# Emitting the S5 table pieces over three projections instead of in one go after the first

## The chip, the core and the metric

One core of a Trainium2 chip runs the whole program. The metric is device time in microseconds (us) of one execution, as the median of several runs; less is better. The engines that matter are TensorE (PE: matmuls, and beside it PEld, its weight loads), VectorE (DVE), ScalarE (ACT), GpSimd (POOL) and SyncE (SP, which issues the weight transfers). Each works through its own list of instructions in order and waits for the others through semaphores.

## The reference, cut to what matters

The program is one layer of a decoder for 256 tokens with 2048 features: a token mixer, cross-attention into a memory, and a gated MLP. Only the mixer's beginning is touched here. It projects the input with one matrix and splits the columns into an S5 state-space group, stick-breaking attention heads, and the heads of a third kind of attention (NSA).

```python
proj = h @ w_in
(u5, sq, sk, sv, nq, kc, vc, ksl, vsl, ksw, vsw, g) = jnp.split(proj, offsets, axis=-1)
y_s5 = s5_mixer(u5, lam_re, lam_im, log_dt, b_re, b_im, c_re, c_im, d, w_glu, b_glu)
y_sb = stick_breaking(heads(sq, SB_HEADS), heads(sk, SB_HEADS), heads(sv, SB_HEADS))
...
# s5_mixer: a complex diagonal recurrence over time, then a gated unit
_, _, sr, si = lax.associative_scan(_complex_affine, (a_r, a_i, xr_in, xi_in), axis=1)
y = einsum(sr, c_re) - einsum(si, c_im) + d * uf
z = jax.nn.gelu(y)
out = z * jax.nn.sigmoid(z @ w_glu + b_glu)
# stick_breaking, per head
w = jnp.where(mask, jnp.exp(jax.nn.log_sigmoid(z) + later), 0.0)
```

The kernel turns the complex recurrence into a real one: it rotates the inputs by a table of cosines and sines over time, runs two real scans with the decay's magnitude, and rotates back. These cosine and sine tables (128 states by 16 groups by 256 steps each) are the "S5 tables".

## The kernel before, in words

Every projection streams its weights from memory in chunks of 512 KB (128 partitions by 1024 numbers; the gates' ones are smaller). `weights` (L272 on) issues the load of a chunk, and `split_chunk` splits it: ScalarE casts a high part (`hi`, L304), VectorE subtracts to get the low part (`lo`, L305). There are four buffers for raw chunks and three each for `hi` and `lo`. Each weight tile then takes three matmuls on TensorE (`mm3`, L319 to L321, with 256 columns, output by features; `mm3x`, L327 to L329, output by tokens): `hi` times the high input, `hi` times the low input, `lo` times the high input. Results lie in three PSUM buffers named `pj`.

The order of the projections: S5's input (`load_x`, 8 chunk pairs); the stick-breaking values (8 chunks, by tokens); queries and keys of the stick-breaking heads (16 chunks: for each of four head pairs t two of queries, two of keys); four column groups for compressed keys and values (8 chunks, `nsa_compress`); NSA values and gates (4 chunks and 8 smaller ones, `nsa_values`); NSA keys (4 + 4 chunks, `nsa_keys`); then the gated unit of S5 (`s5_out`, two chunks of `w_glu`, 48 matmuls from the tiles `s5zs`); then the NSA queries (16 chunks).

Beside them runs a background: the generator `s5_work`, which `step` advances by one piece. `weights` adds `self.pace` to a credit for each chunk and emits a piece for each whole credit. The pieces in order: 4 that build the input matrices (`s5_inputs`: `s5t`, `s5lb`, transposes into `mx`), 32 of the tables (four quarters of 8 pieces: ScalarE fills `Es` and `Ec` with phases, VectorE reduces them in two pieces, ScalarE takes an absolute value and two sines), then 66 of the recurrence. When the first of these last is emitted, the pace becomes 2.8. A state of the recurrence (16 in all) is four pieces: TensorE gives the input product `pb`, VectorE multiplies (`s5m`), adds (`s5z`), scans twice (also into `s5z`), multiplies again and writes `Ec` and `Es`; after every fourth state TensorE forms the output `pa` and VectorE adds it to `s5u`. All have line L191, a helper that issues the engine call and places it behind the latest weight split (VectorE, ScalarE) or a recent projection matmul (TensorE).

The pace is set to 0.8 in `load_x` when its fourth chunk is loaded. After the values, `stick_breaking` has a loop, `while len(self.sins) < 4: self.step()`, that emits all table pieces that are left: 9 of 36 are out by then and 27 follow at once. Then comes the load of ScalarE's table for exponential and logarithm, which has to stand behind the last sine, and the queries and keys. The attention of each head pair t follows (scores in `mx`, `sbe` on ScalarE, `sbs` on VectorE, sums by TensorE into the same `mx`, the weighted values in `op`). `s5_out` emits what is left of the background before it starts on the gelu.

The program names priorities by lane, and a scheduler sets the final order on each engine from these priorities and the dependencies; so a change of where a piece is emitted can move many instructions.

Of the kernel before, what the change touches and what calls it, by code (L numbers as in the profile page):

```python
# [36 lines left out]
SKEW = 16  # L37
MOVING_AT = {512: 48, 256: 32}
NORM0, NORM1, HOLD = 3, (2,), 2
TABLE_PACE, SCAN_PACE = 0.8, 2.8  # L40
BUCKET_FROM = [16, 21, 27, 35, 46, 59, 77, 99, 128, 166, 216]


# [122 lines left out]
class Parts:  # L166
# [9 lines left out]
    def range(self, k, n):  # L176
        if k == 0 and self.first is not None:
            assert n == 1
            return self.first
        return self.tiles[k // self.n][:, k % self.n:k % self.n + n]  # L180
# [18 lines left out]
class Program:  # L199
# [263 lines left out]
    def load_x(self):  # L463

        nc, a, S = self.nc, self.a, self.nc.scalar
        raw = self.slabp.tile([128, KD, 256], F32, name="xraw", tag="Es")
        self.s5u = u = self.s5p.tile([128, 4, 256], F32, name="s5u")
        ps = [self.pj.tile([128, 512], F32, name="pj") for _ in range(3)]
        ps.append(self.op.tile([128, 512], F32, name="op"))
        for c in range(8):  # L470
            s = slice(2 * c, 2 * c + 2)
            with self.lane("split"):
                nc.sync.dma_start(raw[:, s, :], a["xT"][:, s, :])
                self.split_to(self.Xt[:, s, 0, :], self.Xt[:, s, 1, :], raw[:, s, :])
            n = 1 if c == 0 else 2
            for j in range(0, 2, n):
                hi, lo = self.weights(a["win_u"][0, c, :, 512 * j:512 * (j + n)], 512 * n)
                for i in range(n):
                    k = 2 * c + j + i
                    for t in range(4):  # L480
                        w = slice(512 * i + 128 * t, 512 * i + 128 * t + 128)
                        self.mm3(ps[t][:, :256], hi[:, w], lo[:, w], self.X(k, 0), self.X(k, 1),
                                 k == 0, k == KD - 1)
            with self.lane("split"):
                if c == CST_AT:
                    nc.sync.dma_start(self.cst, a["cst"])
                    nc.sync.dma_start(self.bmat, a["s5b"])
                    self.pace = TABLE_PACE
                if c == 7:
                    nc.sync.dma_start(self.cmat, a["s5c"])  # L490

        self.s5us = self.s5p.tile([96, 16, 256], F32R, name="s5us")
        parts = self.Ec[:, 8:16, :].bitcast(F32R).rearrange("p (i t) c -> p i t c", i=2)
        for t in range(4):
            S.copy(u[:, t, :], ps[t][:, :256])
            self.split_to(parts[:, 0, t, :], parts[:, 1, t, :], ps[t][:, :256])
        for j, i in enumerate((0, 1, 0)):
            self.stack(nc.gpsimd, self.s5us[32 * j:32 * j + 32], parts[:, i])

        self.ident16, self.smask16 = (  # L500
            self.s5p.tile([128, 128], mybir.dt.bfloat16, name=f"m16{i}") for i in range(2))
        S.copy(self.ident16, self.ident)
        S.copy(self.smask16, self.smask)
        S.activation(self.nident, self.ident, ACTF.Copy, scale=-1.0)
# [299 lines left out]
    def stick_breaking(self):  # L804
        nc, a, V, S = self.nc, self.a, self.nc.vector, self.nc.scalar
        q = self.sbp.tile([128, 4, 256], F32, name="sbq")
        k = self.sbp.tile([128, 4, 256], F32, name="sbk")
        v = self.sbp.tile([128, 2, 512], F32, name="sbv")
        for i, ps in enumerate(self.to_cols(a["win_sv"][0], self.X, 512, 2, 0, KD)):
            S.copy(v[:, i, :], ps)  # L810
        while len(self.sins) < 4:
            self.step()
        table = self.exp_ln_table(self.sins)
        for t in range(4):
            ps = self.to_rows(a["win_c"], t, self.X)
            S.activation(q[:, t, :], ps, ACTF.Copy, scale=HD ** -0.5)
            ps = self.to_rows(a["win_c"], 4 + t, self.X)
            V.tensor_copy(k[:, t, :], ps)
        self.nsa_bias()
        mm, values = nc.tensor.matmul, []  # L820
        for t in range(4):
            ops = self.op.tile([128, 512], F32, name="op")

            halves = [slice(64 * hh, 64 * hh + 64) for hh in range(2)]
            zs = [self.mx.tile([128, 512], F32, name="mx") for _ in halves]
            row = []
            for c in range(2):
                for z, rows in zip(zs, halves):
                    row.append(mm(z[:, 256 * c:384 if c else 256],
                                  k[rows, t, 128 * c:128 * c + 128], q[rows, t, 128 * c:256],  # L830
                                  start=c == 0, stop=False))
            for z in zs:
                row.append(mm(z[:, 0:128], self.ident16, self.smask16, start=False, stop=False))
                row.append(mm(z[:, 256:384], self.ident16, self.smask16, start=False, stop=True))
            self.in_row(values[-1:] + row)
            ws, exps = [], []
            for z in zs:
                e = self.sbw.tile([128, 384], F32, name="sbe")
                sp = self.sbw.tile([128, 384], F32, name="sbs")
                S.activation(e, z[:, :384], ACTF.Abs)  # L840
                self.after(S.activation(e, e, ACTF.Exp, scale=-1.0), table)
                S.activation(e, e, ACTF.Ln, bias=1.0)
                V.scalar_tensor_tensor(sp, z[:, :384], 0.0, e, ALU.max, ALU.add)
                mm(z[:, 0:384], self.ntri, sp, start=False, stop=False, skip_group_check=True)
                mm(z[:, 128:256], self.nones, sp[:, 256:384], start=False, stop=True,
                   skip_group_check=True)
                w = self.sbw.tile([128, 384], F32, name="sbe")
                exps.append(S.activation(w, z[:, :384], ACTF.Exp))
                self.sb_exp = exps[-1]
                ws.append(w)  # L850
            row = values = []
            for c, (k0, k1) in enumerate(((0, 256), (256, 384))):
                for hh, (w, rows) in enumerate(zip(ws, halves)):
                    h = 2 * t + hh
                    row.append(mm(ops[rows, 128 * c:256], v[:, c, 64 * h:64 * h + 64], w[:, k0:k1],
                                  start=c == 0, stop=c == 1))
            self.tc.add_manual_dep(row[0].ins, exps[1].ins.name, mybir.DependencyInfo(
                mybir.DependencyClass.Sync, mybir.DependencyReason.DATA), reason="side by side")
            self.in_row(row)
            S.copy(self.mix[1][:, t, 0, :], ops[:, :256])  # L860
            V.tensor_sub(self.mix[1][:, t, 1, :], ops[:, :256],
                         self.mix[1][:, t, 0, :].bitcast(F32))
# [507 lines left out]
```

## Time and profile before

| What | us |
|---|---|
| Median of 3 runs | 1277.29 (1276.85 to 1277.38) |
| The profiled execution's own time | 1276.8 |
| Its span in the profile | 1274.6 |
| TensorE busy | 1242.8 |
| TensorE's weight loads busy | 1151.6 |
| VectorE busy | 878.8 |
| ScalarE busy | 660.5 |

The times of the profile are from the start of its span. A busy time counts the union of an engine's instructions; successive instructions overlap by a little, so a row of equal ones is better read from start to start. A group's line names the source line, the engine, the operation, and output and input by the program's names.

### The profile page before, as it was taken

Reading aid. Unit: us, or ns where it says so; the run is one execution under the profiler, and the core shown is the slowest. Engines: PE = TensorE matmul, PEld = TensorE weight load, DVE = VectorE, ACT = ScalarE, POOL = GpSimd, SP = SyncE. Lnnn points to the kernel's source line nnn. Section 1 sums busy time; section 2 is a strip of 40 time slices with the busy share of each in tenths; the row PEclk is TensorE's granted clock in tenths of the full one; section 3 lists DMA queues with packets and bytes.
Section 4 is the critical chain, followed back from the end, with each engine's and each line's share of the span. In section 5 each row is a group of like instructions: output and inputs, shape, how many; then the busy total and the mean of one; then the engine's idle time right before and its main releaser. Section 6 shows DMA issues by size and latency. Waiting matters only on the chain.

```text
span 1274.6 us, 23037 instructions
## 1 busy us (share of the span) xinstructions
PE 1242.8 (98%) x9222; PEld 1151.6 (90%) x9222; DVE 878.8 (69%) x1507; ACT 660.5 (52%) x1032; POOL 19.0 (1%) x34
## 2 busy tenths in 40 slices
PE   7999999999999999899999999999999999999996
PEld 7788889997788999799999999999999988888896
DVE  7799997876765766866666666666666654444557
ACT  6884446565663366365555555555555543334342
POOL 0200000100000000000000000000000000000000
PEclk9999999999999999999999999999999999999998
DMA  8654247664454655355666666666566766656573
GB/s 307 196 167 150 84 130 239 213 197 141 133 204 160 193 196 169 113 164 191 196 192 192 196 193 191 196 194 190 196 192 192 262 192 190 196 188 199 187 237 132
DMA packets 67350, 237.37 MB, mean 186 GB/s; under 512 B 7787, under 2 KB 8604, under 8 KB 66476
## 3 DMA queue, kind: packets, MB, share of 16 engines
q1 hardware_dynamic: 64720, 230.21, 55.9%
q0 software_dynamic: 1424, 4.33, 1.5%
q8 instruction: 72, 1.18, 0.4%
q10 hardware_dynamic: 1100, 1.38, 0.3%
q14 instruction: 34, 0.28, 0.1%
HBM read 231.82 MB, written 2.49 MB: 184 GB/s over the span
## 4 chain that ended last, share of the span: by engine, by line
PE 86%; DVE 6%; DMA 3%; ACT 3%; issue 2%; POOL 0%; DVEq 0%; ACTq 0%; POOLq 0%
PE pj L321 16%; PE pj L319 16%; PE pj L320 16%; PE pj L328 10%; PE pj L327 10%; PE pj L329 10%; PE pa L1081 2%; DVE s5m L191 1%; DVE lo L305 1%; DMA s5us<-Ec 1%; DVE s5z L191 1%; DMA raw<-in_win_u 1%; ACT hi L304 1%; PE mx L1044 1%; PE mx L1045 1%
## 5 line engine op out<-in xcount | busy, mean ns | idle before, releaser
L305 DVE TENSOR_TENSOR lo<-raw,hi 128x1024 fp32r<-128x1024 f32 (+2 forms) x403 | 488.1, 1211 | 330.4 <-ACT hi L304 329.2
L304 ACT CAST hi<-raw 128x1024 fp32r<-128x1024 f32 (+2 forms) x403 | 419.6, 1041 | 500.2 <-PE pj L320 268.1
L320 PE MATMUL pj<-mix,hi 128*128 128x256 f32 x1380 | 382.4, 277 | 0.0
L319 PE MATMUL pj<-mix,hi 128*128 128x256 f32 x1380 | 381.9, 277 | 0.0
L321 PE MATMUL pj<-mix,lo 128*128 128x256 f32 x1380 | 381.3, 277 | 0.0
L319 PEld LDWEIGHTS pj<-mix,hi 128*128 128x128 f32 x1380 | 259.5, 188 | 0.2
L320 PEld LDWEIGHTS pj<-mix,hi 128*128 128x128 f32 x1380 | 259.4, 188 | 0.1
L321 PEld LDWEIGHTS pj<-mix,lo 128*128 128x128 f32 x1380 | 259.4, 188 | 0.0
L319 PE MATMUL pj<-A,hi 128*128 128x256 f32 x496 | 139.6, 284 | 6.7 <-ACT hi L304 6.1
L321 PE MATMUL pj<-A,lo 128*128 128x256 f32 x496 | 137.6, 284 | 3.7 <-DVE lo L305 3.7
L320 PE MATMUL pj<-A,hi 128*128 128x256 f32 x496 | 138.6, 282 | 0.0
L319 PEld LDWEIGHTS pj<-A,hi 128*128 128x128 f32 x496 | 94.4, 191 | 9.4 <-ACT hi L304 6.6
L321 PEld LDWEIGHTS pj<-A,lo 128*128 128x128 f32 x496 | 92.9, 191 | 7.0 <-DVE lo L305 4.9
L328 PE MATMUL pj<-lo,A 128*128 128x512 f32 (+2 forms) x288 | 96.0, 334 | 1.0 <-DVE lo L305 1.0
L328 PE MATMUL pj<-lo,act 128*128 128x512 f32 (+1 forms) x280 | 96.3, 345 | 0.0
L329 PE MATMUL pj<-hi,act 128*128 128x512 f32 (+1 forms) x280 | 96.3, 345 | 0.0
L329 PE MATMUL pj<-hi,A 128*128 128x512 f32 (+2 forms) x288 | 95.8, 334 | 0.0
L320 PEld LDWEIGHTS pj<-A,hi 128*128 128x128 f32 x496 | 94.7, 192 | 0.8 <-issue 0.8
L327 PE MATMUL pj<-hi,A 128*128 128x512 f32 (+2 forms) x288 | 91.4, 334 | 0.6 <-ACT hi L304 0.6
L327 PE MATMUL pj<-hi,act 128*128 128x512 f32 (+1 forms) x280 | 89.3, 345 | 0.0
L328 PEld LDWEIGHTS pj<-lo,A 128*128 128x128 f32 x288 | 54.1, 188 | 7.8 <-DVE lo L305 1.5
L329 PEld LDWEIGHTS pj<-hi,A 128*128 128x128 f32 x288 | 54.2, 188 | 5.8 <-issue 0.8
(321 smaller groups left out, 1792.2 us busy)
## 6 DMA issues: line engine op xcount, KB each, us to landing
raw<-in_w_up SPq DMA_DIRECT2D x176, 512.0 KB, 4.4
raw<-in_w_down SPq DMA_DIRECT2D x92, 512.0 KB, 4.4
raw<-in_win_c SPq DMA_DIRECT2D x48, 512.0 KB, 4.1
raw<-in_w_out SPq DMA_DIRECT2D x32, 512.0 KB, 3.4
raw<-in_win_sv SPq DMA_DIRECT2D x8, 512.0 KB, 4.5
raw<-in_wk_m SPq DMA_DIRECT2D x8, 512.0 KB, 4.1
raw<-in_wv_m SPq DMA_DIRECT2D x8, 512.0 KB, 3.6
raw<-in_wq SPq DMA_DIRECT2D x8, 512.0 KB, 3.4
```

Source lines behind the costliest of these rows:

```text
L191: ins = getattr(self.engine, name)(*args, **kw)
L304: self.last_hi = nc.scalar.copy(hi[:, :n], raw[:, :n])
L305: self.last_lo = nc.vector.tensor_sub(lo[:, :n], raw[:, :n], hi[:, :n].bitcast(F32))
L319: mm(ps, hi, ah, start=start, stop=False)
L320: mm(ps, hi, al, start=False, stop=False)
L321: self.last_mm = mm(ps, lo, ah, start=False, stop=stop)
L327: mm(ps, ah, hi, start=start, stop=False)
L328: mm(ps, ah, lo, start=False, stop=False)
L329: self.last_mm = mm(ps, al, hi, start=False, stop=stop)
L1044: mm(zs, q[:, t, gl, qs], kh[:, 0:m], start=True, stop=False)
L1045: mm(zs, q[:, t, gl, qs], kl[:, 0:m], start=False, stop=True)
L1081: ins = mm(o[64 * r:64 * r + 64, gl, 128 * c:256], vv[:, c, v, :], pt[:, k0:k1], start=start[r] is None, stop=False, skip_group_check=True)
```

## The change

The pace of the pieces becomes a triple: 0.8 from the fourth chunk of `load_x` as before, 1.6 from the values on, 1.8 from the queries and keys on. The loop that emits the rest and the table load for exponential and logarithm move behind the queries and keys. By the pace alone 3 pieces are emitted in `load_x`, 13 in the values and 20 in the first 11 or 12 chunks of the queries and keys, where the tables end and the recurrence begins with its pace of 2.8; so the loop finds nothing left.

```diff
-TABLE_PACE, SCAN_PACE = 0.8, 2.8
+TABLE_PACE, SCAN_PACE = (0.8, 1.6, 1.8), 2.8
...
-                    self.pace = TABLE_PACE
+                    self.pace = TABLE_PACE[0]
...
+        self.pace = TABLE_PACE[1]
         for i, ps in enumerate(self.to_cols(a["win_sv"][0], self.X, 512, 2, 0, KD)):
             S.copy(v[:, i, :], ps)
-        while len(self.sins) < 4:
-            self.step()
-        table = self.exp_ln_table(self.sins)
+        self.pace = TABLE_PACE[2]
         for t in range(4):
             ps = self.to_rows(a["win_c"], t, self.X)
             S.activation(q[:, t, :], ps, ACTF.Copy, scale=HD ** -0.5)
             ps = self.to_rows(a["win_c"], 4 + t, self.X)
             V.tensor_copy(k[:, t, :], ps)
+        while len(self.sins) < 4:
+            self.step()
+        table = self.exp_ln_table(self.sins)
         self.nsa_bias()
```

What stands where in the built programs differs on all engines up to the gated unit; from the NSA queries on TensorE's order is the same for a long way. Lines behind the change are two higher in the new kernel.

VectorE at the end of the values and the start of the queries and keys. Before, from the last two splits of the values on (`lo`; `Es` and `s5lb` are the background):

```order
L305 TENSOR_TENSOR lo<-raw,hi 128x1024 x2
L191 SCALAR_TENSOR_TENSOR Es<-cst,s5v_147,Es 128x256 x4
L191 CAST s5lb<-mx 96x512
L191 TENSOR_SCALAR Es<-Es 128x1024
L191 SCALAR_TENSOR_TENSOR Es<-Es,Ec 128x1024
L191 SCALAR_TENSOR_TENSOR Es<-cst,s5v_147,Es 128x256 x4
L191 TENSOR_SCALAR Es<-Es 128x1024
L191 SCALAR_TENSOR_TENSOR Es<-Es,Ec 128x1024
L191 SCALAR_TENSOR_TENSOR Es<-cst,s5v_147,Es 128x256 x3
L305 TENSOR_TENSOR lo<-raw,hi 128x1024
```

After, from the seventh split of the values on:

```order
L305 TENSOR_TENSOR lo<-raw,hi 128x1024
L191 TENSOR_SCALAR Es<-Es 128x1024
L191 CAST s5lb<-mx 96x512
L305 TENSOR_TENSOR lo<-raw,hi 128x1024
L191 SCALAR_TENSOR_TENSOR Es<-Es,Ec 128x1024
L305 TENSOR_TENSOR lo<-raw,hi 128x1024
L191 SCALAR_TENSOR_TENSOR Es<-cst,s5v_147,Es 128x256 x4
L191 CAST s5lb<-mx 96x512
L191 TENSOR_SCALAR Es<-Es 128x1024
L305 TENSOR_TENSOR lo<-raw,hi 128x1024 x4
```

Eight groups of background work that stood in a row now stand in ones to threes between the splits.

TensorE behind the last matmul of the compressed keys' and values' projections (`pb`, `pa` are the recurrence, `sbs`, `op` and `sbq` the stick-breaking heads, L903 the compression). Before:

```order
L321 MATMUL pj<-A,lo 128x256
L191 MATMUL pb<-s5us,s5lb 128x256 x2
L844 MATMUL mx<-sbs,cst 128x384
L845 MATMUL mx<-sbs,cst 128x128
L191 MATMUL pa<-Ec,s5c 32x256
L903 MATMUL mx<-kv,raw 128x75 x16
L191 MATMUL pb<-s5us,s5lb 128x256 x2
L191 MATMUL pa<-Ec,s5c 32x256
L844 MATMUL mx<-sbs,cst 128x384
L845 MATMUL mx<-sbs,cst 128x128
L327 MATMUL pj<-hi,A 128x256
L855 MATMUL op<-sbe,sbv 64x256 x2
```

After, from the same matmul on:

```order
L321 MATMUL pj<-A,lo 128x256
L191 MATMUL pb<-s5us,s5lb 128x256 x2
L191 MATMUL pa<-Ec,s5c 32x256
L846 MATMUL mx<-sbs,cst 128x384
L847 MATMUL mx<-sbs,cst 128x128
L191 MATMUL pb<-s5us,s5lb 128x256 x2
L191 MATMUL pa<-Ec,s5c 32x256
L846 MATMUL mx<-sbs,cst 128x384
L847 MATMUL mx<-sbs,cst 128x128
L857 MATMUL op<-sbe,sbv 64x256 x2
L857 MATMUL op<-sbe,sbv 64x128 x2
L831 MATMUL mx<-sbq,sbk 128x256 x2
```

Before, only the last head pair's sums are left here; after, the sums of the last two head pairs, with the last pair's scores, and 14 of the compression's 16 products stand between the last pair's two groups of sums.

VectorE at the last output of S5 (`s5u` from `pa`). Before:

```order
L305 TENSOR_TENSOR lo<-raw,hi 128x608
L191 TENSOR_TENSOR Ec<-s5m_2031,s5m_2032 128x256
L191 SCALAR_TENSOR_TENSOR Es<-s5m_2031,s5m_2032 128x256
L305 TENSOR_TENSOR lo<-raw,hi 128x608
L305 TENSOR_TENSOR lo<-raw,hi 128x1024
L191 SCALAR_TENSOR_TENSOR s5u<-s5u,s5prm,pa 128x256
L305 TENSOR_TENSOR lo<-raw,hi 128x1024 x2
L313 TENSOR_TENSOR s5zs<-s5u,s5zs 128x4x256
L305 TENSOR_TENSOR lo<-raw,hi 128x1024
```

After:

```order
L305 TENSOR_TENSOR lo<-raw,hi 128x1024
L968 TENSOR_TENSOR kl_2545<-pj,kh_2544 64x256
L191 TENSOR_TENSOR s5m_2351<-s5z,Ec 128x512
L191 TENSOR_TENSOR s5m_2352<-s5z,Es 128x512
L968 TENSOR_TENSOR kl_2545<-pj,kh_2544 64x256
L191 TENSOR_TENSOR Ec<-s5m_2351,s5m_2352 128x256
L191 SCALAR_TENSOR_TENSOR Es<-s5m_2351,s5m_2352 128x256
L191 SCALAR_TENSOR_TENSOR s5u<-s5u,s5prm,pa 128x256
L1015 TENSOR_SCALAR gate<-gate 128x96
L1016 RECIPROCAL gate<-gate 128x96
L313 TENSOR_TENSOR s5zs<-s5u,s5zs 128x4x256
```

And TensorE there, after:

```order
L321 MATMUL pj<-A,lo 128x256
L191 MATMUL pa<-Ec,s5c 32x256 x2
L191 MATMUL pa<-Es,s5c 32x256 x4
L319 MATMUL pj<-s5zs,hi 128x256 x3
L320 MATMUL pj<-s5zs,hi 128x256
```

Before, the last output comes when the first NSA key chunk has been split, and all 192 matmuls of the key projections stand on TensorE between it and the gated unit; after, it comes behind the splits of all eight key chunks, both of `w_glu` and the first of the NSA queries, with the last key parts (`kl`), and on TensorE the gated unit follows the output at once.

## Rows read from the trace of the kernel before

**Rows 1.** The page's first part: TensorE's busy time, its share of the span, and its instructions.

```profile
PE 1242.8 (98%) x9222; PEld 1151.6 (90%) x9222; DVE 878.8 (69%) x1507; ACT 660.5 (52%) x1032; POOL 19.0 (1%) x34
```

**Rows 2.** Windows: the stretch, its length, then the busy us of TensorE, its weight loads, VectorE, ScalarE and GpSimd with their instructions, the granted clock, the share of DMA and GB/s.

```profile
59.00:102.00 43.00, 39.61 (x300) 36.18 (x300) 41.81 (x67) 34.13 (x47) 1.15 (x2) 0.96 0.55 163
...
155.00:202.00 47.00, 44.89 (x321) 38.51 (x320) 45.24 (x86) 19.85 (x34) 2.57 (x3) 1.00 0.47 145
202.00:224.00 22.00, 22.00 (x196) 22.00 (x195) 14.26 (x18) 16.08 (x29) 1.17 (x2) 1.00 0.80 233
```

**Rows 3.** The timeline of VectorE at the end of the values, and of TensorE where it waits: start, length, instruction, and in brackets the idle time before it with what ended it.

```profile
49.99 1.23 DVE L305 TENSOR_TENSOR lo<-raw,hi 128x1024 fp32r<-128x1024 f32 x1 [1.80 <-ACT hi L304]
...
59.93 1.21 DVE L305 TENSOR_TENSOR lo<-raw,hi 128x1024 fp32r<-128x1024 f32 x1
...
61.20 0.58 PE L321 MATMUL pj<-A,lo 128*128 128x256 f32 x1 [1.63 <-DVE lo L305]
...
72.95 0.38 PE L321 MATMUL pj<-A,lo 128*128 128x256 f32 x1 [0.98 <-DVE lo L305]
...
77.20 0.39 PE L321 MATMUL pj<-A,lo 128*128 128x256 f32 x1 [0.61 <-DVE lo L305]
...
230.55 0.36 PE L319 MATMUL pj<-A,hi 128*128 128x256 f32 x1 [0.60 <-DVE kl L966]
```

**Rows 4.** Windows with a lower granted clock (columns as in rows 2; the clock is the number before the last two).

```profile
61.00:62.00 1.00, 0.80 (x3) 0.80 (x4) 0.97 (x3) 1.00 (x3) 0.00 (x0) 0.59 0.00 0
...
64.00:65.00 1.00, 1.00 (x8) 1.00 (x8) 0.49 (x1) 1.00 (x3) 0.00 (x0) 0.70 0.19 29
...
535.00:538.00 3.00, 3.00 (x16) 2.93 (x17) 2.93 (x5) 1.08 (x4) 0.00 (x0) 0.61 0.05 12
```

**Rows 5.** The timeline of TensorE: the first matmul of the values, the bias table's, the first of the queries and keys, two of the same line 52 steps apart, a group of scores, and an S5 input product.

```profile
33.12 0.48 PE L327 MATMUL pj<-hi,A 128*128 128x512 f32 x1
...
57.70 0.82 PE L874 MATMUL mx<-oh,tab 33*16 33x384 f32 x2
...
59.07 0.39 PE L319 MATMUL pj<-A,hi 128*128 128x256 f32 x1
...
65.07 0.28 PE L319 MATMUL pj<-A,hi 128*128 128x256 f32 x1
...
71.21 0.28 PE L321 MATMUL pj<-A,lo 128*128 128x256 f32 x1
...
148.26 0.92 PE L829 MATMUL mx<-sbq,sbk 64*128 64x256 f32 x8
...
149.64 0.40 PE L191 MATMUL pb<-s5us,s5lb 96*128 96x256 f32 x2
```

**Rows 6.** Windows of VectorE alone: the stretch, its length, VectorE's busy us, the granted clock, DMA.

```profile
34.50:59.90 25.40, 19.43 (x29) 1.00 0.71 189
59.90:145.20 85.30, 82.73 (x139) 0.98 0.48 149
145.20:201.10 55.90, 54.02 (x106) 1.00 0.41 126
```

**Rows 7.** The timeline of VectorE, ScalarE and TensorE from the last S5 output to the gated unit.

```profile
200.63 0.48 DVE L191 SCALAR_TENSOR_TENSOR s5u<-s5u,s5prm,pa 128x256 f32<-128x256 f32 x1 [0.62 <-PE pa L191]
...
201.15 1.06 ACT L778 ACTIVATE s5u<-s5u 128x1024 f32<-128x1024 f32 x1 [0.73 <-DVE s5u L191]
202.23 1.28 ACT L255 ACT_TABLE_LOAD   x1
...
205.19 1.08 ACT L312 CAST s5zs<-s5u 128x1024 fp32r<-128x1024 f32 x1
...
206.30 1.23 DVE L313 TENSOR_TENSOR s5zs<-s5u,s5zs 128x1024 fp32r<-128x1024 f32 x1
...
207.09 0.31 ACT L1012 ACTIVATE gate<-gate 128x96 f32<-128x96 f32 x1
...
223.90 0.28 PE L320 MATMUL pj<-s5zs,hi 128*128 128x256 f32 x1
```

**Rows 8.** VectorE: two groups by form from 32 to 232 (count, busy us, mean ns of one, idle before), then its timeline at three table pieces and at one state of the recurrence with a head's sum in it.

```profile
L305 DVE TENSOR_TENSOR lo<-raw,hi 128x1024 fp32r<-128x1024 f32 x46 | 55.9, 1215 | 14.7 <-ACT hi L304 14.7
...
L966 DVE TENSOR_TENSOR kl<-pj,kh 64x256 fp32r<-64x256 f32 x8 | 3.3, 414 | 0.2
...
51.13 1.67 DVE L191 SCALAR_TENSOR_TENSOR Es<-cst,s5v,Es 128x256 f32<-128x256 f32 x4
...
53.32 0.68 DVE L191 TENSOR_SCALAR Es<-Es 128x1024 f32<-128x1024 f32 x1
53.92 1.22 DVE L191 SCALAR_TENSOR_TENSOR Es<-Es,Ec 128x1024 f32<-128x1024 f32 x1
...
149.27 1.26 DVE L191 TENSOR_TENSOR_SCAN s5z<-s5v,s5z 128x256 f32<-128x256 f32 x2
...
152.98 0.55 DVE L843 SCALAR_TENSOR_TENSOR sbs<-mx,sbe 128x384 f32<-128x384 f32 x1
...
154.78 1.27 DVE L191 TENSOR_TENSOR_SCAN s5z<-s5v,s5z 128x256 f32<-128x256 f32 x2
```

**Rows 9.** The timeline of ScalarE at a half pair's absolute value, and of TensorE at the compression's products with the two groups of sums behind them.

```profile
149.44 0.49 ACT L840 ACTIVATE sbe<-mx 128x384 f32<-128x384 f32 x1 [0.69 <-PE mx L834]
...
156.71 4.42 PE L903 MATMUL mx<-kv,raw 128*128 128x75 f32 x32
...
161.85 0.91 PE L844 MATMUL mx<-sbs,cst 128*128 128x384 f32 x2
```

## The prediction, on record before the change was run

> **What bounds the kernel now.** I read the busy shares first. TensorE is busy for 1242.8 us, 98% of the span [rows 1], so the time moves only where TensorE waits, or stops waiting. I then took the stretch that the change touches, stage by stage [rows 2]: from the start of the queries and keys (59.07) to the gated unit's first matmul (223.78) TensorE has little idle time, but VectorE is hardly less busy: 41.8 of 43.0 us at its beginning, 45.2 of 47.0 up to 202. It has air only from 202 on (14.3 of 22). That is the point to carry along: here the second engine is nearly as full as the first, and work put off on it comes back later.
>
> The stalls that the change aims at are visible. At the end of the values the tables' remaining pieces stand in one lump on VectorE: after the split at 49.99 the next one starts at 59.93, and TensorE waits 1.63 us for it; two chunks later it waits 0.98 and then 0.61 [rows 3]. After the first of these waits the granted clock is 0.5, the lower of its two levels (1.2 instead of 2.4 GHz), until about 64.4 [rows 4]; at half clock for some 3.3 us that is 1.6 us of lost work. The most that the front can give back is 1.63 + 0.98 + 0.61 + 1.6 = 4.8 us.
>
> **The front after the change.** No work is added or removed; pieces move. Table pieces now stand one or two between splits, and nothing shows a split that comes too late, so I take all 4.8 us as gained. I date the front by the end of the 11th of the 16 query and key chunks. The values start at 33.12 and the next stage at 59.07 [rows 5]: 25.95 us. From this go the bias table's matmul (0.82) and the first S5 input product (0.40 each) [rows 5], which now stand later: 24.7. Two table pieces of 0.5 us each now come ahead of or among the casts on ScalarE that the transposes wait for; I put the start 0.5 later, at 33.6. So the queries begin near 58.3. Eleven chunks are 264 matmuls; 52 steps between 65.07 and 71.21 take 0.118 us each [rows 5], after the turn at 202 it is 0.114 (192 matmuls in 21.8 us of rows 2's 22), so 0.116: 30.6. With the bias matmul 0.82, one score group (0.92 for its eight large matmuls, about 1.1 with the small ones), one S5 input 0.40 and 0.8 for switching between kinds [rows 5]: the 11th chunk ends at 92.0. Before, it ends near 101, because by then TensorE has also done four more S5 inputs, three partial outputs and part of the first head pair.
>
> **The bill: VectorE's work that was put off.** The recurrence's steps start only when the tables are finished, now in the 13th chunk where it was the second. VectorE's work from 34.5 to the last S5 output (L191 s5u, 200.63 to 201.12) is 19.43 + 82.73 + 54.02 = 156.2 us, with 10.4 us idle among it [rows 6, 7]. In the new order this last output stands behind ten more weight splits (the other key chunks, both chunks of the gated unit, the first of the NSA queries) at 1.14 from start to start, and eight key splits at 0.40 [rows 8]: 11.4 + 3.2 = 14.6 us more.
>
> Idle time at the front: through the split of the 14th query or key chunk VectorE has, in the new order, 20 weight splits (22.8), the four quarters' table work (1.25 + 1.6 + 0.6 each from start to start, 13.8), three casts, two key copies and small pieces (4.0), two products of the first state (1.2): 41.8 us; for the large pieces see [rows 8]. That split cannot end before 94.2: there are three buffers for the high parts, so it waits for the 11th chunk's end (92.0) plus the cast (1.05) and itself (1.14). From 34.5 that is 59.7 us, so 17.9 us go idle. From there on VectorE has work queued without end: a state costs 149.27 to 154.78 less one 0.47 us piece, 5.0 us [rows 8], 16 of them 80 us, beside the splits.
>
> Idle time later: two of four head pairs now come after the last projection that could run beside them, and there the three engines wait for each other in turn. For the last pair: first half's sums on VectorE, then on TensorE the two sum matmuls (0.9), on ScalarE the weight exponential (0.49, as long as the absolute value of the same tile) and the second half's absolute value, exponential and logarithm (1.6 with their gaps), then VectorE again: 3.0 us, of which its queue covers 0.4; 2.6 idle. Next it needs the compression's 16 products (L903/L905, 4.42 us) [rows 9], of which 14 are queued ahead of the second half's sum matmuls: some 1.5 more. Together 4 us; twice that if TensorE's part runs at the lower clock. I take 6, bounds 0 (all covered) and 12.
>
> The last output then ends at 34.5 + 156.2 + 14.6 + 17.9 + 6 = 229.2 instead of 201.1. Now the chain behind it: gelu 1.06, table load 1.28, the gates' exponential 0.31, high part 1.08, low part 1.23, as they stand in [rows 7], with their small overlaps 4.9 us. In the old order this chain ends at 207.5 and eight key chunks of TensorE work lie over it: 16 us of cover. In the new order all eight are ahead of it, and the next matmuls in TensorE's row read this very result. So the gated unit's second matmul starts near 234.1 against 223.90: +10.2 us. TensorE, some 4 us ahead of the old kernel when it finishes the keys (near 219.5), waits 10 to 15 us there. Take off the 0.60 us for which TensorE now waits for a key split behind the gated unit [rows 3]: those are done long before. Add one spell at the lower clock when the unit starts, 1.6. From there on TensorE's order is the same as before and nothing gives time back: **+11.2 us**.
>
> On the clock, the rows say: lower after a wait of 1.63 us at 61.2 and again at 535.6, not after 0.98 [rows 3, 4]. "TensorE: Matmul & The Clock Gate" of the Trainium skill, Part 1, holds that the array runs at half rate unless recent activity has released it, and that an idle time takes the release back; nothing in it says that a wait as short as 1.63 us should do so, and the trace has that. By the page a wait of 10 us in front of the unit would surely cost a spell; without one my sum would be 9.6.
>
> **The rivals.**
> The **front alone counts**: the S5 chain stays covered and the 4.8 us are kept: 1277.3 - 4.8 = 1272.5, faster. It decides at one point: the last S5 output would have to end by 219, ten us before my date. For it: 22 us of slack between 201.1 and 223.8 [rows 6, 7]. Against: the new order puts 14.6 us of other work ahead, and the front leaves VectorE idle for 17.9 us where it now idles 10.4 all told; together 22.1, with the slack gone before the first wait of the head pairs. 7%.
> **It cancels**: no idle time among the head pairs, the front a little earlier, no clock spell: the last output at 34.5 + 156.2 + 14.6 + 16 = 221.3, the unit's second matmul at 226.2, +2.3 and less the 0.6: +1.7, 1279.0, within 0.2%. 8%.
> **The lower clock sits on the path**: among the head pairs TensorE waits for some us at a time. If it falls to half there, the compression's products take 8.8 instead of 4.42 and the sum matmuls 1.8 instead of 0.9, all of it in the turn-taking that VectorE waits for: 12 us idle instead of 6, and a second spell before it is over: +17 to +19, near 1295. For it: the fall after 1.63 us at 61.2. Against: after waits of 0.5 to 1 us nothing falls. 15%.
>
> **How the numbers follow.** The profiled execution took 1276.8 us (span 1274.6), the median is 1277.29, 0.5 above. 1276.8 + 11.2 + 0.5 = 1288.5, chance 70%. Its own range, with 0 to 10 us idle and one or no spell, is 1281 to 1293; the range takes in the third rival and stops short of the second: 1280.5 to 1297. A difference of 0.2%, 2.6 us, is about what a measurement of this kernel can tell from none. Faster 7%, within it 8%, slower 85%.
>
> **What would show it.** Right: the waits at 59.6, 72.0 and 76.6 are gone from TensorE and the queries begin near 58.3; VectorE's busy share between 59 and 95 falls to some 70%; the last L191 s5u ends near 229 and not 201; the chain of waits holds gelu, table load and the s5zs split; TensorE waits 10 us or more in front of the first s5zs matmul. Wrong: that wait under 4 us, or s5u before 219 (then the front idles less than my 17.9), or new waits of TensorE for hi or lo during the values (then the 92.0 is late, and all after it).

## The result, and the profile after the change

The changed kernel takes 1294.57 us (median of four runs, 1292.41 to 1296.84), the kernel before 1277.07 in the same job: slower by a ratio of 1.0139 (95% interval 1.0127 to 1.0152). The profiled execution is the shortest of the four, 1292.41 us, with a span of 1290.5, 15.9 more than before. The forecast was 1288.5, range 1280.5 to 1297: direction and range hold, and the loss is 17.5 us where 11.2 were forecast. The lines below show what of the sum came as written and which term grew.

**The front** came nearly as predicted. The page's first part, which answers to [rows 1]:

```profile
PE 1245.8 (97%) x9222; PEld 1153.9 (89%) x9222; DVE 879.2 (68%) x1507; ACT 660.3 (51%) x1032; POOL 18.9 (1%) x34
```

TensorE, VectorE and ScalarE run as many instructions as before. TensorE is busy for 3.0 us more and idle for 12.9 us more, so most of the loss is waiting. The queries begin at 59.08 (58.3 predicted), and none of the waits of [rows 3] at their beginning is left. **TensorE's waits** of the changed kernel, from its timeline (start, length, instruction, idle time before it and what ended it):

```profile
59.08 0.28 PE L319 MATMUL pj<-A,hi 128*128 128x256 f32 x1
...
146.79 0.55 PE L191 MATMUL pb<-s5us,s5lb 96*128 96x256 f32 x1 [3.33 <-DVE s5m L191]
...
157.75 3.90 PE L905 MATMUL mx<-kv,raw 128*128 128x75 f32 x28 [0.58 <-ACT sbe L850]
...
164.65 0.38 PE L327 MATMUL pj<-hi,A 128*128 128x256 f32 x1 [1.61 <-ACT hi L304]
...
170.19 0.58 PE L327 MATMUL pj<-hi,A 128*128 128x256 f32 x1 [1.83 <-DVE kv L898]
...
234.29 0.64 PE L191 MATMUL pa<-Ec,s5c 128*32 128x256 f32 x1 [5.99 <-DVE Ec L191]
...
240.40 1.01 PE L319 MATMUL pj<-s5zs,hi 128*128 128x256 f32 x3 [4.19 <-ACT s5zs L312]
241.66 0.58 PE L320 MATMUL pj<-s5zs,hi 128*128 128x256 f32 x1 [0.25 <-DVE s5zs L313]
...
248.51 0.28 PE L319 MATMUL pj<-A,hi 128*128 128x256 f32 x1
```

The last three waits, 10.4 us, are the wait in front of the gated unit that the prediction put at 10 to 15. Those of 3.33, 1.61 and 1.83 us, among the late head pairs and just behind them, it had not on TensorE's account. **VectorE** in windows (stretch, length, busy us, granted clock, DMA), to the end of the last S5 output, which answers to [rows 6]:

```profile
34.50:95.00 60.50, 44.14 (x60) 1.00 0.72 207
95.00:236.73 141.73, 128.51 (x232) 0.93 0.40 131
```

It is busy for 172.7 us and idle for 16.4 in the front and 13.2 behind it; before, 156.2 and 10.4 in all [rows 6, 7]. **The chain behind it**, timelines of VectorE and ScalarE, which answers to [rows 7]:

```profile
236.25 0.48 DVE L191 SCALAR_TENSOR_TENSOR s5u<-s5u,s5prm,pa 128x256 f32<-128x256 f32 x1 [1.68 <-PE pa L191]
236.76 1.06 ACT L778 ACTIVATE s5u<-s5u 128x1024 f32<-128x1024 f32 x1 [3.86 <-DVE s5u L191]
237.84 1.28 ACT L255 ACT_TABLE_LOAD   x1
239.13 0.28 ACT L1014 ACTIVATE gate<-gate 128x96 f32<-128x96 f32 x1
239.32 1.03 ACT L312 CAST s5zs<-s5u 128x1024 fp32r<-128x1024 f32 x1
...
240.38 1.23 DVE L313 TENSOR_TENSOR s5zs<-s5u,s5zs 128x1024 fp32r<-128x1024 f32 x1
```

From the end of the output (236.73) to the unit's second matmul (241.66) it is 4.93 us, as summed: 4.9. The date is what is off, 236.7 in place of 229.2. **Where VectorE idled** behind the front: 1.00, 2.85 and 4.85 us in front of three instructions from 155 to 165, 1.38 at 171.86, 1.68 in front of the last output, the rest in small gaps. The chain of waits (start, length, what), which answers to [rows 9], and the longest of them in VectorE's timeline:

```profile
155.43 0.57 DVE sbs L845
156.04 0.91 PE mx L846 x2
156.95 0.23 PE mx L847 x2
157.21 0.50 ACT sbe L850
157.75 2.34 PE mx L905 x16
160.11 3.42 DMA raw<-in_win_v
163.55 1.05 ACT hi L304
164.63 1.23 DVE lo L305
...
164.63 1.23 DVE L305 TENSOR_TENSOR lo<-raw,hi 128x1024 fp32r<-128x1024 f32 x1 [4.85 <-ACT hi L304]
```

Between VectorE's sum at 155.43 and its split at 164.63 stand the sum matmuls, an exponential, eight of the compression's 16 products (x16: the trace has two rows for each of them), and then a load; in these 9.2 us VectorE has only two other instructions, of 0.47 and 0.56 us. The first chunk of win_v1 takes a buffer that these products still read, so it starts at 160.11 and VectorE's split gets its high part only at 164.6, with S5 pieces queued behind that split. **The clock**, windows of TensorE (stretch, length, busy us, granted clock), which answers to [rows 4]:

```profile
146.00:152.00 6.00, 4.62 (x12) 0.50 0.00 0
...
166.00:173.00 7.00, 5.17 (x24) 0.52 0.44 153
...
232.00:244.00 12.00, 5.27 (x24) 0.50 0.32 87
244.00:246.00 2.00, 2.00 (x16) 0.81 0.00 0
```

Three spells at the lower level in place of one. The last reaches into the gated unit, to about 244.8; the unit takes 8.27 us (240.40 to 248.67) where it took 6.16 (223.78 to 229.94).

### The profile page after: what moved, and what is told of

Read it like the earlier page. It is cut to its first block, busy times and chain, and to the rows that moved or that the text cites. A ratio compares the mean times of both kernels' runs of the same rounds, so it can differ in the third digit from the quotient of the medians.

```text
span 1290.5 us, 23022 instructions
## 1 busy us (share of the span) xinstructions
PE 1245.8 (97%) x9222; PEld 1153.9 (89%) x9222; DVE 879.2 (68%) x1507; ACT 660.3 (51%) x1032; POOL 18.9 (1%) x34
## 3 DMA queue, kind: packets, MB, share of 16 engines
q8 instruction: 72, 1.18, 0.4%
q10 hardware_dynamic: 1100, 1.38, 0.3%
## 4 chain that ended last, share of the span: by engine, by line
PE 91%; DVE 5%; DMA 2%; ACT 1%; issue 1%; SPq 0%; DVEq 0%; ACTq 0%
PE pj L321 17%; PE pj L319 17%; PE pj L320 17%; PE pj L327 11%; PE pj L328 10%; PE pj L329 10%; PE pa L1083 2%; DMA raw<-in_win_u 1%; DVE s5m L191 1%; DVE lo L305 1%; PE mx L1046 1%; PE mx L1047 1%; PE pa L191 1%; DVE s5z L191 1%; ACT hi L304 1%
## 5 line engine op out<-in xcount | busy, mean ns | idle before, releaser
L321 PEld LDWEIGHTS pj<-A,lo 128*128 128x128 f32 x496 | 92.1, 189 | 3.2 <-issue 1.6
```

The costliest lines, as they stand in the source:

```text
L321: self.last_mm = mm(ps, lo, ah, start=False, stop=stop)
```

## The experiments

Theory A is the prediction's: VectorE's put-off S5 work ends after TensorE has run out of other work, and the chain behind it is bare. Rival C: it is the late head pairs (their exp table is loaded after the keys) and the clock. First, parts of the change.

**The spread over the values alone**: the changed kernel with the loop and the table load back behind the values:

```diff
-        self.pace = TABLE_PACE[2]
+        while len(self.sins) < 4:
+            self.step()
+        table = self.exp_ln_table(self.sins)
         for t in range(4):
...
-        while len(self.sins) < 4:
-            self.step()
-        table = self.exp_ln_table(self.sins)
```

> The pace of 1.6 in the values is kept, the loop that emits the rest stands behind the values again (20 pieces in one go there instead of 27). Theory A (what costs is that the recurrence, and with it the heads, start ten chunks later; spreading itself is good): no loss at all, and a part of the front's 4.8 us is gained: 1273 to 1276 against 1277. Rival B (spreading in the values itself delays the weight splits): slower, 1279 or more.

1276.10 us, ratio 0.9995 (0.9987 to 1.0004): no change. Rival B falls, and the part gain that theory A expected is not shown. The wait of 1.64 us only moves, from 59.6 to 68.2 behind a split of the queries, and a spell at the half clock follows at 75. The rest of the pieces still stands in one lump.

**The pieces in the queries too, but at pace 4.0**, loop and table load behind the queries and keys as in the change: `TABLE_PACE = (0.8, 1.6, 4.0)`.

> The changed kernel with a pace of 4.0 instead of 1.8 from the queries and keys on: the tables end in the 5th chunk of them, the first state stands behind the 6th split and not the 13th (3rd before), the last S5 output behind 39 splits (37 before, 47 in the change). Theory A: the loss goes and the front's gain stays: 1271 to 1275. Rival B (the moved loop or the spreading is bad as such, whatever the pace): 1285 or more.

1278.64 us, ratio 1.0009 (1.0000 to 1.0018). The loss is gone, as theory A said, and the front's gain, which it expected too, does not show. TensorE reaches the first sums of the head pairs at 90.04, 2.35 us ahead of the kernel before (92.39), and loses that to two waits for VectorE (timeline) and the spells behind them (windows):

```profile
152.65 0.59 PE L846 MATMUL mx<-sbs,cst 128*128 128x384 f32 x1 [1.64 <-DVE sbs L845]
168.70 0.36 PE L191 MATMUL pb<-s5us,s5lb 96*128 96x256 f32 x1 [1.64 <-DVE s5m L191]
...
154.00:162.00 8.00, 7.42 (x35) 0.50 0.20 66
170.00:174.00 4.00, 4.00 (x23) 0.57 0.23 51
```

**The kernel before with the recurrence late, the head pairs on time:**

```diff
+        self.pace = 0.0
         for t in range(4):
+            if t == 3:
+                self.pace = 2.8
```

> The kernel before, tables in one go behind the values, heads as they were, but the recurrence's first piece held back until 12 chunks of queries and keys are emitted: S5 late, heads in time. Theory A (main cost: VectorE's put-off recurrence ends behind the key projections, and TensorE waits in front of the gated unit): 1286 to 1291, with a wait of 8 us or more before the first s5zs matmul. Rival C (main cost: the last two head pairs without projections beside them): 1276 to 1280.

1293.23 us, ratio 1.0122 (1.0103 to 1.0140). A fourth execution took 6233 us, which nothing in the traces explains; median and ratio are without it. This is nearly the whole loss, from the S5 work alone, and somewhat more than theory A's 1286 to 1291. The last output ends at 235.24, and TensorE waits 2.67, 5.37 and 4.19 us in front of the unit (timeline); below it VectorE's windows:

```profile
232.81 0.63 PE L191 MATMUL pa<-Ec,s5c 128*32 128x256 f32 x1 [5.37 <-DVE Ec L191]
...
238.91 0.80 PE L319 MATMUL pj<-s5zs,hi 128*128 128x256 f32 x2 [4.19 <-ACT s5zs L312]
...
34.50:95.00 60.50, 40.92 (x57) 0.97 0.66 188
95.00:235.24 140.24, 133.02 (x237) 0.98 0.44 143
```

Rival C falls as the main cause, and so do the spells among the head pairs: up to 228 the clock is low here only from 75 to 79. VectorE idles for 26.8 us up to its last output, about as long as in the changed kernel (29.6), but 19.6 of them lie before 95, where the S5 work is held back. So it is the late S5 work that costs, and the idle time among the head pairs is only one way in which VectorE loses time.

**The kernel before with the head pairs late, S5 on time** (the exp table's load waits for the third pair's queries):

```diff
-        table = self.exp_ln_table(self.sins)
...
+        table = self.exp_ln_table(self.sins + [late])
```

> The kernel before with S5 as it was, but the table load for exponential and logarithm, and so all heads, held until the third pair's queries are done (as late as in the change). Theory A: only the waits of the head pairs come, 3 to 7 us more than before: 1280 to 1284, no wait in front of the gated unit. Rival C: nearly the whole loss, 1289 to 1295.

1287.95 us, ratio 1.0091 (1.0078 to 1.0105): between the two. The last S5 output is early (196.64), and the loss is TensorE's own: 5.3 us more of waits from 20 to the unit's beginning (12.2 against 6.9), and a spell after the largest, in timeline and windows:

```profile
162.01 0.63 PE L191 MATMUL pa<-Ec,s5c 128*32 128x256 f32 x1 [3.59 <-DVE Ec L191]
...
162.00:176.00 14.00, 13.41 (x54) 0.50 0.12 39
```

13.4 us of work at half clock are an estimated 6.7 us lost. So the head pairs have a price of their own, some 11 us, and it does not add to the 16 of S5: together they make 17.5. That fits two delays that run at the same time, with the unit waiting for the later one.

**Less work on VectorE**, in the changed kernel and in the kernel before:

```diff
-            V.tensor_tensor_scan(z[:, 1], mg, z[:, 1], 0.0, ALU.mult, ALU.add)
```

> The changed kernel without the second of the two scans of each S5 state (the scan of the imaginary part is left out, so its S5 outputs are other numbers): 16 scans of 0.63 to 0.67 us, some 10.3 us less work on VectorE ahead of the last S5 output, nothing else. Theory A (VectorE's total of work and idle time up to the last S5 output sets when the gated unit begins): the last S5 output comes 8 to 10 us sooner, and the time falls by as much as TensorE waited for it, 5.99 + 4.19 us at most less what stays of the chain: 1284 to 1288. Rival C (the loss is TensorE's own, the spells at the half clock and the late head pairs, and VectorE has slack): 1291 to 1295.

> The kernel before without the second scan of each S5 state (left out as in the run beside it, with other S5 outputs for it): 10.3 us less work on VectorE, which there ends the S5 outputs 23 us before TensorE asks for them. Theory A: no change, 1275 to 1278. If this kernel gains as much as the changed one does, the gain says nothing of the changed order.

The changed kernel falls to 1284.98 us (1282.54 to 1286.04), ratio 1.0058 to before (1.0046 to 1.0070): 9.6 less, for 10.3 us of VectorE's work. Its last output ends at 228.98, 7.8 sooner, and the unit begins 3.93 us behind it; the two profiled executions differ by 7.0. Its half clock before the unit is shorter too (table below), so the gain need not be VectorE's work alone. The kernel before, though, becomes slower, 1282.66, ratio 1.0044 (1.0029 to 1.0059), with less to do. This was not expected, and it spoils the control: the scans left out also changed the order, TensorE met a wait of 2.12 us (timeline) and a long spell (windows):

```profile
159.19 0.36 PE L191 MATMUL pb<-s5us,s5lb 96*128 96x256 f32 x1 [2.12 <-DVE s5m L191]
...
162.00:174.00 12.00, 11.42 (x45) 0.50 0.30 99
```

**A dose between**, pace 2.6 in the queries and keys: `TABLE_PACE = (0.8, 1.6, 2.6)`, otherwise as at 4.0.

> The changed kernel with a pace of 2.6 in the queries and keys: in VectorE's order the first S5 state then follows 9 weight splits (13 in the changed kernel, 6 at a pace of 4.0, 3 before), the last S5 output 45 (47, 39, 37), and the head pairs' sums stand almost where they stood before. Theory A (what counts is how much of the S5 work is put off behind the last splits): the last output stands 6 of the 8 splits that lie between a pace of 4.0 and the change, so three quarters of the 16 us between these two, 1287 to 1291. Rival D (the late head pairs start the loss, and with them on time the S5 work finds room): 1276 to 1281.

1276.72 us, ratio 0.9998 (0.9989 to 1.0007): theory A's number is missed by 10 us. I had made the loss proportional to the splits ahead of the last output. It is a maximum: the output now ends at 219.85, 18.7 us later than before, and costs almost nothing, because TensorE reaches the unit only at 223.50.

```profile
219.38 0.47 DVE L191 SCALAR_TENSOR_TENSOR s5u<-s5u,s5prm,pa 128x256 f32<-128x256 f32 x1
...
224.73 0.50 PE L319 MATMUL pj<-s5zs,hi 128*128 128x256 f32 x2 [1.23 <-ACT s5zs L312]
```

That is the point that the prediction named for its first rival: an output by 219 is covered. Rival D has the number, but not its reason: with the heads on time and the S5 work late, above, nearly the whole loss came.

**The high part ahead of the exp table's load:**

```diff
-        self.table = self.exp_ln_table(self.gelus)
-        self.split_to(zs[:, :, 0, :], zs[:, :, 1, :], z)
+        high = S.copy(zs[:, :, 0, :], z)
+        self.table = self.exp_ln_table(self.gelus + [high])
+        V.tensor_sub(zs[:, :, 1, :], z, zs[:, :, 0, :].bitcast(F32))
```

> The changed kernel with the high part of s5zs cast ahead of the load of the exp table, 1.28 us, and the gates' exp. Theory A with the prediction's third step (the chain from the last S5 output over gelu, table load, cast and subtraction to the gated unit is exposed, 4.9 us of it): the gated unit begins 1.0 to 1.6 us sooner, 1292.5 to 1293.8. Rival (the exp of the gates, the table or VectorE's subtraction hold the unit all the same): no change, 1294 to 1295.

1295.04 us, ratio 1.0148 (1.0134 to 1.0162), no gain. The chain did become shorter (the unit's first matmul starts 2.21 us after the last output ends, 3.67 before), but the unit then took 9.31 us in place of 8.27: it began 1.0 earlier within a spell that lasted until 246.

**A wait of TensorE filled**, in the kernel with pace 2.6, ahead of the last pair's first sum:

```diff
+                if t == 3 and z is zs[0]:
+                    for _ in range(4):
+                        row.append(mm(ops[:, 0:256], self.ntri, k[:, 0, :], start=True, stop=True))
```

> The kernel with a pace of 2.6 in the queries and keys, and four matmuls of 128x256 whose result is thrown away on TensorE ahead of the first sum of the last head pair, where it waited 1.62 us for VectorE at 149.25 and then ran from 153.4 to 163.4 at the half clock. Theory A with its clock term (that wait brings the spell, and the spell's 4.6 us are TensorE's path there): the spell is gone or shorter, and the time is 1272 to 1274.5. Rival (the spell comes all the same, or what TensorE gains it waits for VectorE's last S5 output, which ends only 4.9 us ahead of the gated unit): 1275.5 to 1278.

1276.90 us, ratio 1.0001 (0.9992 to 1.0010): the rival. TensorE has no wait over 0.58 between 60 and 221, the spell comes all the same though shorter, and what is gained (the unit is reached at 221.66, not 223.50) is waited for VectorE. A timeline and windows, of the longest of its eleven executions (1279.99):

```profile
225.87 0.54 PE L319 MATMUL pj<-s5zs,hi 128*128 128x256 f32 x2 [4.21 <-ACT s5zs L312]
...
152.00:154.00 2.00, 2.00 (x17) 1.00 0.00 0
154.00:156.00 2.00, 2.00 (x14) 0.63 0.39 119
156.00:160.00 4.00, 4.00 (x12) 0.50 0.60 210
```

**The idle time among the head pairs filled**, in the changed kernel, with recurrence pieces emitted ahead of win_v1's first chunk:

```diff
+        for _ in range(4):
+            self.step()
+        self.credit -= 4
+        self.holds = [self.es]
         for i, ps in enumerate(self.to_cols(a["win_v1"][0], self.X, 256, 4, 0, KD)):
```

> The changed kernel with four pieces of the recurrence, some 5 us of VectorE's work, emitted ahead of the first chunk of the weights win_v1 (and not again later): in VectorE's order they now stand ahead of the head pairs' last sum and of the split that waited 4.85 us for its chunk. Theory A (the 7 us by which the prediction fell short are VectorE's idle time there, which it spent with S5 work queued behind the waiting instruction): the last S5 output comes 3 to 5 us sooner, 1289 to 1292. Rival (the pieces hold the last head pair up, and the idle time moves behind it): 1293 to 1296.

1296.75 us, ratio 1.0146 (1.0131 to 1.0162): the rival. The pieces hold up the last pair, TensorE waits 2.68 us for them, falls to half clock, runs 14 of the compression's products (x28) in 6.25 us instead of 3.90, and the load comes later by that. VectorE's idle time moves behind the pieces, in timelines of TensorE and VectorE:

```profile
162.40 6.25 PE L905 MATMUL mx<-kv,raw 128*128 128x75 f32 x28 [0.58 <-ACT sbe L850]
...
163.87 0.56 DVE L845 SCALAR_TENSOR_TENSOR sbs<-mx,sbe 128x384 f32<-128x384 f32 x1 [2.54 <-ACT sbe L844]
170.59 1.23 DVE L305 TENSOR_TENSOR lo<-raw,hi 128x1024 fp32r<-128x1024 f32 x1 [6.17 <-ACT hi L304]
```

**TensorE's two waits in front of the unit filled**, in the changed kernel:

```diff
+            if t == 0:
+                fill = [nc.tensor.matmul(ps[:, :256], hi[:, 0:128], hi[:, 256:512], start=True,
+                                         stop=True) for _ in range(34)]
+                self.after(fill[20], self.pa_last)
+                self.in_row(fill)
```

> The changed kernel with 34 matmuls of 128x256 whose result is thrown away on TensorE in its two waits ahead of the gated unit: 20 in the 5.99 us for the last state, 14 in the 4.19 us behind the last S5 output. Theory A with its clock term (TensorE's idle time there brings the 13.6 us at the half clock, and these cost the gated unit 2.1 us): the gated unit takes 6.2 to 6.5 us in place of 8.3, and the time is 1291.5 to 1293.5. Rival (the unit waits on VectorE and ScalarE within itself): no change, 1294 to 1296.

The unit does run at the full clock (timeline and window of TensorE):

```profile
243.63 0.62 PE L319 MATMUL pj<-s5zs,hi 128*128 128x256 f32 x3 [0.92 <-ACT s5zs L312]
...
244.00:250.00 6.00, 5.36 (x45) 1.00 0.01 3
```

It takes 6.92 us in place of 8.27, with a wait of 0.64 in it. TensorE still waits 3.42 us for the last state and is at half clock from about 239.4 to 242.8, but this spell ends before the unit. The time does not follow: 1297.65 us, ratio 1.0163 (1.0149 to 1.0177). In the profile TensorE ran at half clock from 164 to 185, far ahead of the fill, and the last S5 output ended at 239.96. Whether the fill has to do with that was the next question.

**The changed kernel once more**, unaltered.

> The changed kernel itself once more. In the run with the filled waits TensorE ran at the half clock from 164 to 185, far ahead of the fill and in an order that is the same up to there, and the last S5 output came 3.2 us later than in the first profile of the changed kernel. Theory E (the length of these spells differs between executions of one program, and the S5 work goes with it): times spread over 1292 to 1297 as before, and the last S5 output in this profile lies between 235 and 241, later the longer the spells ahead of it. Rival (the fill itself does it, through the program's code or its weights): times and profile agree with the first profile within 1 us, the last S5 output at 236 to 237.5.

1295.41 us (1292.50 to 1296.73), ratio 1.0138 (1.0114 to 1.0162). This profiled execution took 1296.68; windows of TensorE:

```profile
146.00:156.00 10.00, 8.70 (x38) 0.52 0.00 0
168.00:182.00 14.00, 12.33 (x58) 0.50 0.46 153
```

and of VectorE, to the end of the last S5 output:

```profile
34.50:95.00 60.50, 44.09 (x59) 1.00 0.73 210
95.00:241.54 146.54, 129.03 (x232) 0.88 0.40 127
```

One program, the same front, the same work on VectorE; the first spell lasts some 10 us instead of 6 and the second 14 instead of 7, VectorE idles 17.5 us instead of 13.2, the last output ends 4.8 later and the span is 4.2 longer. So a spell like that of the run before comes without a fill. Why all four times of that run (1296.54 to 1300.42) lie in the upper part of the changed kernel's, or above, stays open.

The profiles side by side; the half clock, in us, is summed over the full windows of 1 us from 20 to the unit's beginning:

| kernel | last S5 output ends | unit begins | unit takes | half clock before it | median |
|---|---|---|---|---|---|
| before | 201.12 | 223.78 | 6.16 | 3.4 | 1277.1 |
| pace 4.0 | 207.77 | 227.19 | 6.18 | 13.6 | 1278.6 |
| pace 2.6 | 219.85 | 224.73 | 7.90 | 10.2 | 1276.7 |
| changed, one scan | 228.98 | 232.91 | 8.34 | 8.3 | 1285.0 |
| S5 late | 235.24 | 238.91 | 7.96 | 12.5 | 1293.2 |
| changed | 236.73 | 240.40 | 8.27 | 22.6 | 1294.6 |
| changed, again | 241.54 | 245.21 | 7.91 | 37.2 | 1295.4 |
| heads late | 196.64 | 234.54 | 6.16 | 20.5 | 1288.0 |

With S5 late and in both profiles of the changed kernel the unit's first matmul starts 3.67 us after the output, each time: there VectorE sets the time. With the heads late the output is early and the unit late: there it is TensorE, by its waits and its clock. No version is faster than the kernel before by more than the noise: the front can give back 4.8 us at most, and in the versions where TensorE came earlier it waited later.

## Why the prediction was right, and which terms were too small

- **The front**: right, with some luck: the values start at 34.33, 0.7 later than the 33.6 assumed, and the 11 chunks with what lies between them take 33.0 us instead of 33.7. So the 11th chunk ends at about 92.1 (92.0). VectorE idles 16.4 us between 34.5 and 95 (17.9), its busy share from 59 to 95 is 67% (70). That this gain does not reach the end is shown by the kernels with pace 4.0 and 2.6 and by the filled wait.
- **The put-off work**: right in kind, and shown by the late S5 alone; the paces and the scan left out agree. In size, 172.7 us of work ahead of the last output's end against 170.8.
- **The idle time among the head pairs**: the step that was too small. 6 us with bounds of 0 and 12; VectorE idles 13.2 us behind the front in one execution and 17.5 in the other. In the first, 10.1 of them lie at the last pair and just behind it (1.00, 2.85, 4.85, 1.38). The prediction counted the turn-taking of sums, exponentials and products, and not the load behind the products: 3.42 us in which a chunk of win_v1 comes into a buffer that they had to release, then its cast. The 4.85 us of VectorE's wait for it are most of the 7.2 that were missing. That the load costs time of its own was read from the chain; no run gave the load another buffer, so it is not shown what the time would be without it.
- **The chain behind the output**: right, 4.93 against 4.9.
- **The clock**: too small. 1.6 us in the unit were 2.1, and the spells among the head pairs stood in the third rival only. That rival (the lower clock on the path, 12 us idle, near 1295, given 15%) is nearest to what was measured, and without it the prediction's own range of 1281 to 1293 would have missed the median. The rival's mechanism is seen in the kernel with pieces ahead, where the products take 6.25 us instead of 3.90 (1.6 times, not the double that it was priced at). In the changed kernel it holds in part: the last pair's products at 157.75 ran at the full clock, and there the turn-taking and the load made the idle time. The third pair's sums just ahead and, in the second execution, the compression's second 16 products (6.94 us instead of 4.32) ran in a spell.
- **The sum** of the likeliest case, with the measured work and idle times, is 229.2 + 1.9 - 1.5 + 7.2 = 236.8 for the output: the whole 7.5 us by which it came later than forecast.
- **TensorE's own date**: the keys end at 227.8, not 219.5. The waits of 3.33, 1.61 and 1.83 us and the first two spells were missing from it. It did not decide, since VectorE was later still; the late heads alone show what it would have cost.
- Of the +18.0 us at the first matmul behind the unit (248.51 against 230.55), 15.9 are left at the end of the span, so the "nothing gives time back" of the sum was 2.1 too strict. About 1.0 of it is a wait of 0.97 us for VectorE at 268.95, which the kernel before has and the changed kernel does not; the rest was not followed.

Against the third rival the prediction held that nothing falls after waits of 0.5 to 1 us, and its rows do not bear that out. The fall at 535 [rows 4] stands in the kernel before behind waits of 1.18, 0.68, 0.86 and 0.35 us, none of them near 1.63:

```profile
530.62 0.99 PE L1200 MATMUL mx<-mix,nident 128*128 128x384 f32 x2 [1.18 <-ACT mix L1199]
...
534.31 0.30 PE L1191 MATMUL mx<-cst,R 128*128 128x128 f32 x1 [0.86 <-DVE R L1182]
```

On the clock the prediction cited "TensorE: Matmul & The Clock Gate" of the Trainium skill, Part 1, for a spell after a long wait in front of the unit. The trace agrees (0.50 from 232 to 244, with the waits of 5.99 and 4.19 us in it), and with those waits filled, though not wholly, the unit ran at 1.00.

## What to carry to other kernels

When two engines are nearly full, moving work from one stage to a later one on the second engine is free only up to the date at which the first asks for its result: compute that date as a maximum (here 219 to 220 for the last S5 output), not as a cost for each piece moved. Where a chain passes between three engines, follow the buffers too: a load that can start only when the last reader has let go belongs into the chain with its full latency. And look at what a stall does to the clock before pricing it at its own length.

## What the runs showed of the hardware that was not expected

- The spells at half clock differ between executions of one program: 166 to 173 in one, 168 to 182 in the other, with a span that is 4.2 us longer. The changed kernel's spread from 1292.4 to 1296.8 goes with the mean granted clock of its runs (0.985 and 0.984 at the lower times, 0.981 and 0.980 at the upper).
- A wait does not decide alone. The clock fell after waits of 1.62 to 1.64 us in several kernels, but with the S5 work late it stayed up after one of 1.64 at 61.7 and fell at 75, behind waits of 1.43 and 0.76; in the kernel before it fell at 535 behind waits of 0.35 to 1.18; with the wait filled it fell at 154.5, with no wait over 0.58 ahead, while TensorE ran the compression's products of 75 columns.
- A kernel with 10 us less work on VectorE was 5.5 us slower; its profile has a wait of 2.12 us that the kernel before does not have, and some 13 us at half clock behind it.
